# Down projection of the second and third token block by seven products of block sums, woven into the gate and up products

## Chip, core and metric

The kernel runs on one core of one Trainium2 chip. The time is the device time of one execution in microseconds (us); smaller is better. The program computes one layer of a decoder for a prompt of 2048 positions and a group of 32 sample rows (8 sequences of 4 positions).

## The reference, cut to what matters

The layer is attention beside a gating unit, an output projection with residual, and then a SwiGLU feed-forward part with residual, to which the change belongs:

```python
D_MODEL = 1024
D_FF = -(-8 * D_MODEL // (3 * 256)) * 256      # 2816

def _swiglu(x, g, w_gate, w_up, w_down):
    h = _rmsnorm(x, g)
    return (jax.nn.silu(h @ w_gate) * (h @ w_up)) @ w_down

def _layer_prompt(x, ...):
    ...
    x = x + jnp.concatenate([att, u * gate], axis=-1) @ w_out
    x = x + _swiglu(x, norm2_g, w_gate, w_up, w_down)
```

Everything is float32. `_layer_sample` does the same for the sample rows with the same weights, and a last RMSNorm follows. The caches of the sample group are copied to the outputs, shifted by the new positions.

## The kernel before

About the first 1000 us are projection and attention. The rest is done in three blocks of row tiles (a row tile is 128 positions): tiles 0 to 5, 6 to 11, and 12 to 15 with the sample rows. Each block first does the output projection and the second norm (the transition), and then the feed-forward part, in NF = 22 passes over f, each for 128 of the 2816 columns of `w_gate` and `w_up`.

**Precision.** A matmul operand is split into a high part (rounded to the matmul's float32 form) and a low part (the rest): `hi = copy(x)` on ScalarE (ACT), `lo = x - hi` on GpSimd (POOL) or VectorE (DVE). A product is three matmuls: high x high, high x low, low x high.

**Gate and up.** They are computed together as a 2x2 by 2x2 block product with seven products instead of eight (Strassen's way, in Winograd's form): rows in two halves of 64, `w_gate` and `w_up` against two halves of the inner dimension. For each f there are seven operand tiles (four blocks or sums of blocks of the weights), and seven `product(B, u, q)`, q = 0 to 6, of 12 matmuls each (4 parts k of the inner dimension, three matmuls each). They move 384 columns in block 2 (6 tiles x 64) and 272 in block 3 (4 tiles x 68, the sample rows with them). After a product, DVE or ACT combines its result from PSUM with earlier ones; silu stands on ACT after q = 2 and q = 5; after q = 6 `hidden` multiplies gate and up and splits the result as the stationary operand of the down projection. The first block forms the operand sums and keeps them in DRAM (`ab_d`); the others load them from there (`load_source`, tile names `fr`).

**The tick.** One product with what is issued behind it is a tick: `one(u, q)`. The order of all engines' instructions is that of the code (a manual schedule); each engine works its own queue in that order. In a tick of blocks 2 and 3, `prepare(B, f + 1, q)` issues for the next pass the low half of operand q - 1 (POOL, L1604), the high half of operand q (ACT, L1600) and the load of operand q of the pass after that (the SP queue). `later(n, ...)` puts work n ticks ahead.

**Down.** For each f, 128 rows of `w_down` are loaded into one row tile `fd` (`load_down`) and split into a pair `dw` (`split_down`, ACT L135 and POOL L138, 1024 wide). Two passes, an even and an odd f, make one `down_unit` for each row tile: for each of two 512-column halves 2 x 3 matmuls (L1743) into one PSUM bank and a DVE addition to the accumulator in SBUF (`acc`, L1745). These units stand in the ticks q = 3, 4 and 5 of the next even pass, two tiles each in block 2; the sample rows have a unit of 8 matmuls.

Of the kernel before, what the change touches and what calls it, by code (L numbers as in the profile page):

```python
# [19 lines left out]
P = 128  # L20
# [45 lines left out]
def hymba_step(ctx: ExitStack, tc: tile.TileContext, A: dict, O: dict):  # L66
# [53 lines left out]
    ab_d = dram.tile([NF, 7, P, 512], F32, name="ab_d")  # L120

# [1163 lines left out]
    def op_tile():  # L1285

        t_ = pool_["fg"].tile([P, 2, 512], F32R, name="op", tag="op", bufs=8)
        return t_[:, 0], t_[:, 1]
# [37 lines left out]
    class Block:  # L1326
# [9 lines left out]
        def place(self):  # L1336
            self.X = []
            for nm in ("xh2", "xl2"):
                t_ = fc.tile([P, 6 * 28 * 64], F32R, name=nm, tag=nm)
                self.X.append(t_[:, 0:self.nt * 28 * self.w].rearrange("p (i n) -> p i n", i=self.nt))  # L1340
            self.ops = [x.rearrange("p i (j k w) -> p i j k w", j=7, k=4) for x in self.X]
# [207 lines left out]
    ab, ops = {}, {}  # L1549
    POOL_LOW = (2, 4, 5)  # L1550
# [47 lines left out]
    def high(f, j):  # L1598
        ops[f, j] = op_tile()
# [6 lines left out]
    def both_halves(f, j):  # L1606
# [12 lines left out]
    EVEN_STAGES = (((both_halves, 0), (keep, 3)), ((both_halves, 1), (keep, 1)), ((both_halves, 2),), ((both_halves, 3),),  # L1619
                   ((sums, 5), (both_halves, 4)), ((both_halves, 5),), ((both_halves, 6), (keep, 5)), (), ())  # L1620
# [20 lines left out]
    def load_down(f):  # L1641
        raws["d", f] = w_ = pool_["fd"]
        sync.dma_start(w_, A["w_down"][f * P:(f + 1) * P, :])

# [6 lines left out]
    def product(B, u, q):  # L1651
# [9 lines left out]
        for k in range(4):  # L1661
# [3 lines left out]
            pe.matmul(out, wl[:, ks], xh[:, :, k], start=False, stop=(k == 3))  # L1665

# [28 lines left out]
        elif q == 6:  # L1695
            if a == 0:
# [16 lines left out]
    def hidden(B, u, zz, c):  # L1713

        f, a, b, g = u["f"], u["a"], u["b"], u["g", zz]
        dve.tensor_mul(g, g, c)  # L1716
# [9 lines left out]
        return lows  # L1726

# [102 lines left out]
    for s in range(KD):  # L1830
        at(L + (-12 if s < 4 else s - 14), "misc", lambda s=s: load_wo(0, s, lambda: first_stage(s)))
        at(L + (s - 11 if s < 4 else s - 10), "misc", split_wo, B, 0, s, lambda s: op_tile())
# [18 lines left out]
    gain.append(row_tile("final_g"))  # L1851
    pool_["fd"] = row_tile("fd")
# [24 lines left out]
    def first_operands(B):  # L1877
# [6 lines left out]
        later(6, load_down, 0)  # L1884
# [30 lines left out]
    def first_block(B):  # L1915
# [21 lines left out]
        def rest():  # L1937
# [3 lines left out]
            sync.dma_start(gain[0], dap(A["final_g"], 0, [[0, P], [1, D]]))  # L1941
# [33 lines left out]
    def next_block(B, downs, finals):  # L1975
# [15 lines left out]
        for s in (6, 7):  # L1991
            later(s - 5, split_wo, B, 0, s, lambda s: op_tile())
# [14 lines left out]
    for bi, B in enumerate(blocks):  # L2007
        if bi == 0:
# [10 lines left out]
        last_h = {}  # L2019

        def one(u, q):
            tick()
            product(B, u, q)
            f = u["f"]
# [5 lines left out]
            if f and q < 2:  # L2030
                prepare(B, f, 7 + q)
            if f + 1 < NF:
# [166 lines left out]
```

## Time and profile before

| | |
|---|---|
| time, median of 3 runs | 2595.95 us (2592.98 to 2599.67) |
| the profiled execution: time, span | 2594.14 us, 2592.3 us |
| TensorE (PE) busy, matmuls | 2467.8 us (95%), 13598 |
| weight loads (PEld) busy | 2175.4 us (84%) |
| DVE, ACT, POOL busy | 1430.4 us (55%), 1221.5 us (47%), 1369.7 us (53%) |
| mean granted TensorE clock | 0.985 |
| stages: feed-forward of block 1, 2, 3 | about 1030 to 1520, 1620 to 2100, 2200 to 2560 us |

How to read the profile: PE's matmuls are pipelined, so that one matmul's own length is longer than the distance to the next one's start; the distance is what it costs. In the views, `op<-fr` is an operation that writes tile `op` from tile `fr`; L1604 is line 1604 of the kernel; `[0.81 <-PE ps_m L1665]` is the idle time of that engine ahead of an operation and what ended it. Each engine takes its instructions in order, so an instruction that waits holds all behind it. In the groups by line, the numbers behind the second bar are the idle time ahead of the group and what ended most of it. SPq is the queue that issues DMA transfers.

### The profile page before, as it was taken

To read this page: it belongs to the slowest core of one execution; us is meant where nothing else is said; L and a number is where in the kernel's file an instruction comes from. 1 tells how busy PE (TensorE), PEld (TensorE's weight loads), DVE (VectorE), ACT (ScalarE), POOL (GpSimd) and SP (SyncE) were. 2 spreads that over 40 slices of the span, in tenths; PEclk is the share of its full clock that TensorE was granted. 3 is DMA by queue.
4 is the path that set the end of the run, shared out by engine and by line. 5 is a ranking of instruction groups with operands and counts; after the bars stand their busy time and mean duration, and the time that the engine had idled before them with its cause. 6 is when DMAs were issued, how large, how long until landed. Compare 5 with 4: busy or idle time off the path is not lost.

```text
span 2592.3 us, 38968 instructions
## 1 busy us (share of the span) xinstructions
PE 2467.8 (95%) x13598; PEld 2175.4 (84%) x13598; DVE 1430.4 (55%) x2783; ACT 1221.5 (47%) x2578; POOL 1369.7 (53%) x1068
## 2 busy tenths in 40 slices
PE   8998899999999889999999999999999999999996
PEld 6777776677988768898999988999999987999996
DVE  3359686345888877344444466544444457544445
ACT  5423335446878745554454545432332336444332
POOL 2035654123576745776776743554453634766662
PEclk9999999999999999999999999999999999999998
DMA  7764853588678674464564564455463643755553
GB/s 236 226 204 150 272 159 117 180 247 276 195 223 219 175 210 150 143 206 156 163 195 134 183 187 159 171 187 175 151 215 126 210 154 127 239 194 196 195 195 109
DMA packets 313409, 480.00 MB, mean 185 GB/s; under 512 B 25841, under 2 KB 178834, under 8 KB 307326
## 3 DMA queue, kind: packets, MB, share of 16 engines
q1 hardware_dynamic: 307740, 468.48, 56.7%
q10 hardware_dynamic: 5474, 9.04, 1.3%
q8 instruction: 108, 1.77, 0.3%
q14 instruction: 87, 0.71, 0.1%
HBM read 381.72 MB, written 165.83 MB: 211 GB/s over the span
## 4 chain that ended last, share of the span: by engine, by line
PE 36%; issue 8%; POOL 8%; DMA 4%; ACT 2%; DVE 2%; SPq 1%; POOLq 0%; ACTq 0%; DVEq 0%
PE ps_o L1743 12%; PE ps_m L1665 8%; PE ps_m L1663 8%; PE ps_m L1664 8%; POOL op L1604 2%; DMA ab_d<-pair 2%; ACT fr L1572 1%; POOL pair L1584 1%; POOL dw L138 1%; POOL fr L1587 1%; POOL pair L1593 1%; POOL pair L1590 1%; DMA out_yp_dram<-acc 1%; SPq L1390 1%; PE ps_o L1411 0%
## 5 line engine op out<-in xcount | busy, mean ns | idle before, releaser
L1604 POOL TENSOR_TENSOR op<-fr,op 128x512 fp32r<-128x512 f32 x385 | 488.6, 1298 | 285.1 <-ACT op L1600 273.9
L1665 PE MATMUL ps_m<-xh,op 128*128 128x384 f32 (+5 forms) x1932 | 610.8, 316 | 2.0 <-POOL op L1604 2.0
L1663 PE MATMUL ps_m<-xh,op 128*128 128x384 f32 (+5 forms) x1932 | 610.9, 316 | 0.0
L1664 PE MATMUL ps_m<-xl,op 128*128 128x384 f32 (+5 forms) x1932 | 609.8, 316 | 0.0
L1743 PE MATMUL ps_o<-dw,hw 128*128 128x512 f32 x2040 | 485.8, 393 | 14.8 <-DVE acc L1745 14.8
L1743 PEld LDWEIGHTS ps_o<-dw,hw 128*128 128x128 f32 x2040 | 380.5, 188 | 98.4 <-DVE acc L1745 21.9
L1663 PEld LDWEIGHTS ps_m<-xh,op 128*128 128x128 f32 x1932 | 364.2, 189 | 4.0
L1664 PEld LDWEIGHTS ps_m<-xl,op 128*128 128x128 f32 x1932 | 364.2, 189 | 3.5
L1665 PEld LDWEIGHTS ps_m<-xh,op 128*128 128x128 f32 x1932 | 364.1, 188 | 2.5 <-POOL op L1604 2.5
L1745 DVE TENSOR_TENSOR acc<-acc,ps_o 128x512 f32<-128x512 f32 (+1 forms) x362 | 247.1, 687 | 214.8 <-PE ps_o L1743 214.7
L1710 ACT ACTIVATE ps_t<-zn 128x384 f32<-128x384 f32 (+1 forms) x126 | 58.2, 462 | 463.9 <-DVE zn L1693 364.5
L1600 ACT ACTIVATE op<-fr 128x512 fp32r<-128x512 f32 x396 | 235.5, 623 | 20.8 <-DMA fr<-ab_d 18.1
L138 POOL TENSOR_TENSOR dw<-fd,dw 128x1024 fp32r<-128x1024 f32 x66 | 158.5, 2402 | 120.1 <-ACT dw L135 119.4
L318 PE MATMUL ps_s<-wh,xh 128*128 128x512 f32 x480 | 197.2, 411 | 6.1 <-ACT xh L135 6.0
L319 PE MATMUL ps_s<-wl,xh 128*128 128x512 f32 x480 | 191.7, 399 | 2.0 <-DVE wl L226 2.0
L320 PE MATMUL ps_s<-wh,xl 128*128 128x512 f32 x480 | 191.5, 399 | 0.0
L1604 POOL TENSOR_TENSOR op<-pair,op 128x512 fp32r<-128x512 f32 x63 | 81.2, 1297 | 117.1 <-ACT op L1600 117.1
L1720 ACT ACTIVATE hw<-ps_t 128x384 fp32r<-128x384 f32 (+1 forms) x126 | 56.1, 453 | 175.1 <-DVE ps_t L1716 174.1
L318 PEld LDWEIGHTS ps_s<-wh,xh 128*128 128x128 f32 x480 | 92.5, 193 | 35.9 <-issue 8.4
L319 PEld LDWEIGHTS ps_s<-wl,xh 128*128 128x128 f32 x480 | 92.8, 193 | 20.8 <-DVE wl L226 3.6
L320 PEld LDWEIGHTS ps_s<-wh,xl 128*128 128x128 f32 x480 | 92.2, 192 | 20.4 <-DVE xl L138 0.2
L135 ACT ACTIVATE dw<-fd 128x1024 fp32r<-128x1024 f32 x66 | 69.8, 1057 | 73.1 <-DMA fd<-in_w_down_dram 73.1
(489 smaller groups left out, 4769.6 us busy)
## 6 DMA issues: line engine op xcount, KB each, us to landing
fr<-ab_d SPq DMA_DIRECT2D x308, 256.0 KB
fd<-in_w_down_dram SPq DMA_DIRECT2D x66, 512.0 KB
out_ks_dram<-in_cache_k_dram SPq DMA_DIRECT2D x56, 512.0 KB
out_vs_dram<-in_cache_v_dram SPq DMA_DIRECT2D x56, 512.0 KB
ab_d<-fr SPq DMA_DIRECT2D x88, 256.0 KB
raw<-in_w_in_dram SPq DMA_DIRECT2D x72, 256.0 KB
qk_d<-pair SPq DMA_DIRECT2D x64, 256.0 KB
ab_d<-pair SPq DMA_DIRECT2D x63, 256.0 KB
```

Source lines behind the costliest of these rows:

```text
L135: act.activation(hi, src, AF.Copy)
L138: (eng_lo or pool).tensor_sub(lo, src, hi.bitcast(F32))
L318: pe.matmul(o[j], xh[:, k, :], wh, start=(k == 0), stop=False)
L319: pe.matmul(o[j], xh[:, k, :], wl, start=False, stop=False)
L320: pe.matmul(o[j], xl[:, k, :], wh, start=False, stop=(k == KD - 1))
L1600: act.activation(ops[f, j][0], ab[f][j], AF.Copy)
L1604: (pool if f or j in POOL_LOW else dve).tensor_sub(lo_, ab[f][j], hi.bitcast(F32))
L1663: pe.matmul(out, wh[:, ks], xh[:, :, k], start=(k == 0), stop=False)
L1664: pe.matmul(out, wh[:, ks], xl[:, :, k], start=False, stop=False)
L1665: pe.matmul(out, wl[:, ks], xh[:, :, k], start=False, stop=(k == 3))
L1743: pe.matmul(ps[0:nr], l_, r_[:, cs], start=(z == 0 and y == 0), stop=(z == FC - 1 and y == len(pairs) - 1))
L1745: dve.tensor_add(B.acc[i][0:nr, cs], B.acc[i][0:nr, cs], ps[0:nr])
```

## The change

From the second block on, the down projection is also made by seven products of block sums. The first block forms the sums of the blocks of `w_down` (`block_sums`, four DVE subtractions for each pair of passes) and keeps them in a DRAM tensor `td_d`; for this there are now two row tiles (`fd`, `fe`) instead of one and a separate one for the final gain, whose load moves to the end of each block. In blocks 2 and 3 a class `Seven` does the down projection of the pairs of passes 0 to 9; the last pair stays as it was.

A pair of passes gives 256 hidden rows, so the left side is 2x2 blocks (two row tiles by two passes) and the right side 2x2 blocks (two passes by two 512-column halves). `hidden` now multiplies gate and up on DVE into e1, e2 (even f) and o1, o2 (odd f), from which DVE forms sums; `put` splits the seven left blocks (high on ACT; low on DVE, for one block on POOL), `split` the seven right blocks (`d`, 512 wide: 0, 2 and 4 low on DVE, 1, 3, 5 and 6 low on POOL, and in block 3 also 7, for the sample rows). A step is 3 matmuls of 512 columns into a PSUM bank, in which products are added up, and a DVE addition of the bank to `acc` (7 for each pair of row tiles, where the units had 4). Two banks take turns.

In what follows, O0 to O6 are the ticks of an odd pass and E0 to E6 those of the even pass after it. The steps of a pair of passes are woven in from E3 on, one behind each part k of a product, so 4 in a tick: 21 in block 2 (to O1) and 14 with 4 for the sample rows in block 3 (to O0). The down units between the ticks are gone in blocks 2 and 3. `prepare` stands three ticks later there: the low half of operand j is issued three ticks ahead of the product that reads it. The operand buffers, a ring of 8, are a ring of 5 and one of 3 from which three right blocks are also taken.

```diff
-        t_ = pool_["fg"].tile([P, 2, 512], F32R, name="op", tag="op", bufs=8)
+        t_ = pool_["fg"].tile([P, 2, 512], F32R, name="op", tag="ox" if extra else "op", bufs=3 if extra else 5)
...
-    EVEN_STAGES = (((both_halves, 0), (keep, 3)), ((both_halves, 1), (keep, 1)), ((both_halves, 2),), ((both_halves, 3),),
-                   ((sums, 5), (both_halves, 4)), ((both_halves, 5),), ((both_halves, 6), (keep, 5)), (), ())
+    EVEN_STAGES = ((), ((both_halves, 0), (keep, 3)), ((both_halves, 1), (keep, 1)), ((both_halves, 2),), ((both_halves, 3),),
+                   ((sums, 5), (both_halves, 4)), ((both_halves, 5),), ((both_halves, 6), (keep, 5)), ())
...
+    def block_sums(g, part):
+        (t1, t3), (t4, t2) = ((r_[:, 0:512], r_[:, 512:1024]) for r_ in (rows2[1], rows2[0]))
+        if part == 0:
+            dve.tensor_sub(t1, t3, t1)
+        elif part == 1:
+            dve.tensor_sub(t3, t2, t3)
+            dve.tensor_sub(t2, t2, t1)
+            dve.tensor_sub(t4, t4, t2)
...
             pe.matmul(out, wl[:, ks], xh[:, :, k], start=False, stop=(k == 3))
+            if woven:
+                woven(k)
...
+        def split(self, eng, *ds):
+            for d in ds:
+                hi, lo_ = self.d[d]
+                act.activation(hi, self.raw(d), AF.Copy)
+                eng.tensor_sub(lo_, self.raw(d), hi.bitcast(F32))
+
+        def put(self, key, src, eng):
+            hi, lo_ = self.a[key]
+            act.activation(hi, src, AF.Copy)
+            eng.tensor_sub(lo_, src, hi.bitcast(F32))
...
+        def even(self, part):
+            e1, e2 = self.h[0]
+            if part == 0:
+                self.put("11", e1, dve)
+                self.h[2] = s3 = zn_tile()[:, 0:self.n]
+                dve.tensor_sub(s3, e1, e2)
+            else:
+                self.put("s3", self.h[2], dve)
+        def odd_a(self):
+            (e1, e2), (o1, o2) = self.h[0], self.h[1]
+            dve.tensor_sub(e1, e2, e1)
+            hi, lo_ = self.a["12"]
+            dve.tensor_sub(lo_, o1, hi.bitcast(F32))
+            self.put("s2", e1, dve)
...
+        STEPS = (("11", 0, 0, (0, 0)), ("12", 1, 1, (0, 0)), ("s2", 2, 0, (0, 1)), ("s1", 3, 1, (1, 1)), ("s3", 4, 0, (1, 1)),
+                 ("s4", 5, 1, (0, 1)), ("22", 6, 0, (1, 0)))
...
+        def one(self, p, banks, step):
...
+            for x, (l_, r_) in enumerate(((ah, dh), (ah, dl), (al, dh))):
+                pe.matmul(ps, l_, r_, start=(new and x == 0), stop=(x == 2), skip_group_check=True)
+            acc = self.B.acc[2 * p + par][:, half * 512:(half + 1) * 512]
+            dve.tensor_add(acc, acc, ps)
...
+        def plan(self, f, q):
+            g = f // 2
+            if f % 2 and g + 1 < NF // 2:
...
+                if q in (2, 3):
+                    self.even(q - 2)
+                if q in (1, 2, 4):
+                    self.load(g, *{1: (0, 1, 2, 3), 2: (4, 6), 4: (5, 7) if self.B.last else (5,)}[q])
+                for eng, ds in {2: ((dve, (0,)), (pool, (1,))), 3: ((dve, (2,)),), 4: ((pool, (3,)),),
+                                5: ((dve, (4,)),), 6: ((pool, (5,)),)}.get(q, ()):
+                    self.split(eng, *ds)
+            elif f % 2 == 0 and f:
+                if q == 0:
+                    self.split(pool, 6)
+                if q == 2 and self.B.last:
+                    self.split(pool, 7)
...
-            product(B, u, q)
+            product(B, u, q, st and st.woven(f, q))
+            if st and u["b"] == B.nt:
+                st.plan(f, q)
...
-            if f and q < 2:
-                prepare(B, f, 7 + q)
-            if f + 1 < NF:
-                prepare(B, f + 1, q)
+            if st:
+                if f and q < 5:
+                    prepare(B, f, 4 + q)
+                if f + 1 < NF and q > 2:
+                    prepare(B, f + 1, q - 3)
```

TensorE's queue in block 2 before, at a tick with two down units (L1743; `ps_o` are the down units' banks):

```order
L1663 MATMUL ps_m_16820<-xh_15482,op 128x384
L1664 MATMUL ps_m_16820<-xl_15483,op 128x384
L1665 MATMUL ps_m_16820<-xh_15482,op 128x384
L1743 MATMUL ps_o_16841<-dw,hw 128x512 x6
L1743 MATMUL ps_o_16849<-dw,hw 128x512 x6
L1743 MATMUL ps_o_16857<-dw,hw 128x512 x6
L1743 MATMUL ps_o_16865<-dw,hw 128x512 x6
L1663 MATMUL ps_m_16873<-xh_15482,op 128x384
```

and now, at E3 (`ao` and `pair` are left blocks; `op` and `db` right blocks):

```order
L1683 MATMUL ps_m_16920<-xh_15563,op 128x384
L1898 MATMUL ps_o_16924<-op,ao 128x512 x3
L1681 MATMUL ps_m_16920<-xh_15563,op 128x384
L1682 MATMUL ps_m_16920<-xl_15564,op 128x384
L1683 MATMUL ps_m_16920<-xh_15563,op 128x384
L1898 MATMUL ps_o_16932<-op,ao 128x512 x3
```

The down matmuls moved from between the products into them, three behind each part of a product.

POOL's queue in block 2 before, over two passes (L138 splits a row tile of `w_down`, L1604 is the low half of a gate and up operand):

```order
L1604 TENSOR_TENSOR op<-fr,op 128x512 x6
L138 TENSOR_TENSOR dw<-fd,dw 128x1024
L1604 TENSOR_TENSOR op<-fr,op 128x512 x4
L138 TENSOR_TENSOR dw<-fd,dw 128x1024
L1604 TENSOR_TENSOR op<-fr,op 128x512 x10
```

and now (L1607 is the low half of a gate and up operand, L1811 that of a right block, L1816 that of left block 22); the first L1811 is issued at O2, the last at E0:

```order
L1607 TENSOR_TENSOR op<-fr,op 128x512 x8
L1811 TENSOR_TENSOR op<-fd,op 128x512
L1607 TENSOR_TENSOR op<-fr,op 128x512 x2
L1811 TENSOR_TENSOR db<-db 128x512
L1607 TENSOR_TENSOR op<-fr,op 128x512 x2
L1811 TENSOR_TENSOR db<-fd,db 128x512
L1607 TENSOR_TENSOR op<-fr,op 128x512
L1811 TENSOR_TENSOR db<-db 128x512
L1607 TENSOR_TENSOR op<-fr,op 128x512
L1816 TENSOR_TENSOR ao<-zn,ao 128x384
```

Two long splits in a pair of passes became four short ones and a left block, which stand between the last low halves of the odd pass and the first five of the even one.

ACT's queue in block 2 at the same place, now, from O0 to O4 (L1693 takes the first product from PSUM, L1730 is silu, L1603 the high half of a gate and up operand, L1815 that of a left block, L1810 that of a right block):

```order
L1693 ACTIVATE zn<-ps_m_17945 128x384
L1603 ACTIVATE op<-fr 128x512 x2
L1730 ACTIVATE ps_t_18025<-zn 128x384
L1815 ACTIVATE ao<-fe 128x384
L1810 ACTIVATE op<-fd 128x512 x2
L1603 ACTIVATE op<-fr 128x512
L1815 ACTIVATE ao<-zn 128x384
L1810 ACTIVATE op<-op 128x512
```

where before stood, over the same ticks:

```order
L1673 ACTIVATE zn<-ps_m_17010 128x384
L1600 ACTIVATE op<-fr 128x512 x2
L1710 ACTIVATE ps_t_17065<-zn 128x384
L1600 ACTIVATE op<-fr 128x512 x2
L135 ACTIVATE dw<-fd 128x1024
L1600 ACTIVATE op<-fr 128x512
```

Behind silu, a left block and two right blocks now stand ahead of the next high half.

More of the change, by code (lines that the diff above doesn't have):

```diff
@@ L1598, in high @@
     def high(f, j):
-        ops[f, j] = op_tile()
+        ops[f, j] = op_tile(f == 0 and j > 4 if seven else j in (2, 5))
         act.activation(ops[f, j][0], ab[f][j], AF.Copy)
@@ L2018, in hymba_step @@
         rows = list(range(len(B.rows)))
-        last_h = {}
+        st = Seven(B) if bi else None
+        for u in units:
+            u["seven"] = st if u["f"] + 2 < NF else None
         def one(u, q):
+            f = u["f"]
             tick()
-            product(B, u, q)
-            f = u["f"]
+            if st and f and f % 2 == 0 and q == 3:
+                st.begin(f // 2 - 1)
+            product(B, u, q, st and st.woven(f, q))
+            if st and u["b"] == B.nt:
+                st.plan(f, q)
             if u["b"] < B.nt:
```

190 lines of the change are left out of this document (171 added, 19 removed).

## Prediction

> **What bounds the kernel now.** I read the busy time by stage first, then the timeline of TensorE in blocks 2 and 3, then the groups by line of those stretches. In the windows (stretch, its length, then PE, PEld, DVE, ACT, POOL busy us, granted clock, DMA share, GB/s; one row each from block 2 and block 3):
>
> ```profile
> 1700.00:1750.00 50.00, 50.00 (x267) 47.07 (x266) 22.38 (x39) 16.67 (x31) 26.72 (x21) 1.00 0.56 190
> 2300.00:2350.00 50.00, 50.00 (x328) 45.71 (x327) 24.82 (x54) 18.06 (x41) 26.70 (x19) 1.00 0.52 174
> ```
>
> PE has no gap there; the other engines are busy about half the time. What PE's time is made of, by the timeline (start, length, what):
>
> ```profile
> 1699.79 0.33 PE L1663 MATMUL ps_m<-xh,op 128*128 128x384 f32 x1
> ...
> 1707.42 0.33 PE L1665 MATMUL ps_m<-xh,op 128*128 128x384 f32 x1
> 1707.59 5.64 PE L1743 MATMUL ps_o<-dw,hw 128*128 128x512 f32 x24
> 1713.07 0.33 PE L1663 MATMUL ps_m<-xh,op 128*128 128x384 f32 x1
> ...
> 2306.10 0.29 PE L1663 MATMUL ps_m<-xh,op 128*128 128x272 f32 x1
> ...
> 2307.60 1.98 PE L1743 MATMUL ps_o<-dw,hs 128*64 128x512 f32 x8
> ```
>
> Starts are what counts. From 1699.79 to 1707.59 stand 45 matmuls: 173 ns each in block 2. The 24 down matmuls take 5.48 us: 228 ns each. In block 3, 12 gate and up matmuls fill 2306.10 to 2307.60: 125 ns each. So one of the seven products (12 matmuls, a tick) is 2.08 us in block 2 and 1.50 us in block 3, and a pair of passes 168 x 0.173 + 72 x 0.228 = 45.5 us in block 2, 168 x 0.125 + 56 x 0.228 = 33.8 us in block 3 (with the 8 of the sample rows).
>
> **What is removed.** Twelve matmuls for each row tile and pair of passes become 21 for two row tiles, so 3 are saved per pair of tiles: 9 in block 2 (2.05 us) and 6 in block 3 (1.37 us) for each of ten pairs of passes, 150 x 228 ns = 34.2 us. All of it is on the path, since PE has no gap. The sample rows stay at 8.
>
> **What is moved and added: the queues behind PE.** The groups by line of block 2 (line, engine, shapes, count, busy us, mean ns):
>
> ```profile
> L1604 POOL TENSOR_TENSOR op<-fr,op 128x512 fp32r<-128x512 f32 x136 | 172.5, 1299 | 153.4 <-ACT op L1600 143.9 <-DMA fr<-ab_d 8.9
> L1745 DVE TENSOR_TENSOR acc<-acc,ps_o 128x512 f32<-128x512 f32 x120 | 82.6, 688 | 80.0 <-PE ps_o L1743 80.0
> L1600 ACT ACTIVATE op<-fr 128x512 fp32r<-128x512 f32 x136 | 80.8, 622 | 0.6
> L1720 ACT ACTIVATE hw<-ps_t 128x384 fp32r<-128x384 f32 x40 | 19.7, 493 | 77.9 <-DVE ps_t L1716 77.1
> L1710 ACT ACTIVATE ps_t<-zn 128x384 f32<-128x384 f32 x39 | 19.4, 496 | 224.4 <-DVE zn L1693 172.0 <-DVE zn L1677 52.4
> L1677 DVE TENSOR_TENSOR zn<-zn,ps_m 128x384 f32<-128x384 f32 x19 | 10.5, 554 | 27.7 <-PE ps_m L1665 27.7
> ```
>
> and of block 3:
>
> ```profile
> L1716 DVE TENSOR_TENSOR ps_t<-ps_t,raw 128x272 f32<-128x272 f32 x40 | 17.8, 446 | 15.7 <-ACT ps_t L1710 15.0
> L1710 ACT ACTIVATE ps_t<-zn 128x272 f32<-128x272 f32 x40 | 15.9, 397 | 133.0 <-DVE zn L1693 115.2 <-DVE zn L1677 17.7
> L1720 ACT ACTIVATE hw<-ps_t 128x256 fp32r<-128x256 f32 x40 | 15.4, 385 | 27.5 <-DVE ps_t L1716 27.5
> L1677 DVE TENSOR_TENSOR zn<-zn,ps_m 128x272 f32<-128x272 f32 x20 | 8.8, 438 | 17.3 <-PE ps_m L1665 17.2
> L1324 DVE TENSOR_TENSOR hs<-ps_t,hs 128x16 fp32r<-128x16 f32 x38 | 6.3, 165 | 0.0
> L1716 DVE TENSOR_TENSOR raw<-raw,zn 128x136 f32<-128x136 f32 x1 | 0.3, 299 | 1.1 <-ACT raw L1710 1.1
> ```
>
> How POOL hangs on PE shows in this chain of block 3, begun by the product that ended at 2307.60:
>
> ```profile
> 2307.80 0.44 DVE L1693 TENSOR_TENSOR zn<-zn,ps_m 128x272 f32<-128x272 f32 x1 [0.81 <-PE ps_m L1665]
> 2308.27 0.40 ACT L1710 ACTIVATE ps_t<-zn 128x272 f32<-128x272 f32 x1 [10.73 <-DVE zn L1693]
> 2308.61 0.62 ACT L1600 ACTIVATE op<-fr 128x512 fp32r<-128x512 f32 x1
> 2309.30 1.29 POOL L1604 TENSOR_TENSOR op<-fr,op 128x512 fp32r<-128x512 f32 x1 [8.16 <-ACT op L1600]
> ```
>
> PE to DVE 0.20, then silu, then ACT's next high half, then POOL. Before, such a low half was used some six ticks later, and the down units, 5.5 us each, lay among those ticks. After, `prepare` runs three ticks later, so that a low half is issued three ticks ahead of its product; down splits stand before it in the same queues, and from O1 to E2 nothing is woven in: ticks of 2.08 and 1.50 us. I follow the last finisher at four places, block 2 / block 3.
>
> *O5 needs low half 5 at its third matmul.* After O2: 0.20 + add 0.554 / 0.438 + silu 0.496 / 0.397 + high half of block 11 0.493 / 0.385 + two split highs 1.24 + POOL's split and low half 5, 2 x 1.299 = 5.6 / 5.3. PE has two ticks and two matmuls, 26 x 0.173 or 0.125 = 4.5 / 3.25. Wait 1.1 / 2.0.
>
> *E0 needs low half 0.* Three POOL operations after low half 5, 3.90, against two ticks: 0 / 0.9.
>
> *E2 needs low half 2.* After O5: add, silu, split 4 on ACT and DVE (about 0.69, as an add) 2.56 / 2.35; the hidden products on DVE, two pairs of half size (128x136 took 299 ns and 128x272 446, so 0.36 / 0.29 each) and an add, with two small sample operations in block 3, 1.99 / 1.94; a small ACT step 0 / 0.17; ACT's block 12 and split 5, 1.11 / 1.01; POOL 2.60. Sum 8.3 / 8.1 against 38 matmuls, 6.6 / 4.75, and the 0.9 already waited. Wait 1.7 / 2.4.
>
> *E3 needs low half 3.* Two POOL operations 2.60 less one tick: 0.5 / 1.1.
>
> In block 2 the woven step at O0 also waits for DVE: the hidden work of E6 (1.99) stands before the add that frees its bank: 0.684 + 0.20 + 0.69 + 1.99 + 0.69 = 4.25 against 3.6 on PE, 0.6. Elsewhere a bank comes back in time: one 0.69 add against 1.2 us of PE.
>
> Together 3.9 / 6.4 us for a pair of passes, more than the 2.05 / 1.37 saved.
>
> **A price from another stage.** Nearly all the new DVE operations read two SBUF tiles; the removed and the kept ones read PSUM. Where such operations meet POOL:
>
> ```profile
> 957.14 0.68 DVE L1403 TENSOR_TENSOR xl<-xl,xh 128x512 fp32r<-128x512 f32 x1
> ...
> 959.45 3.47 DVE L138 TENSOR_TENSOR woh<-fr,woh 128x512 fp32r<-128x512 f32 x2
> ...
> 958.94 1.74 POOL L1086 TENSOR_TENSOR o<-o,zn 128x512 f32<-128x512 f32 x1
> ```
>
> 0.68 alone; in turns with POOL each takes 1.7, and POOL's 1.30 becomes 1.7 too. So every low half that meets one loses 0.40 (512 wide), by width 0.30 at 384 and 0.20 at 256. The bounds are 0 (they pass between POOL's operations) and 0.40; I take the width, since thirteen come for each pair of passes: six POOL operations in the waits of block 2, 1.8; eight in block 3, 1.6.
>
> **Transfers.** A 512 KB load in block 3:
>
> ```profile
> 2316.50 0.33 SPq L1643 DMA_DIRECT2D fd<-in_w_down_dram  x1
> ...
> 2320.03 1.06 ACT L135 ACTIVATE dw<-fd 128x1024 fp32r<-128x1024 f32 x1 [2.41 <-DMA fd<-in_w_down_dram]
> ```
>
> It landed 3.5 us after issue. The loads of O1 stand on SP behind an operand load that waits for low half 3: in block 3 that ends 5.4 us after E6's product (sample step 0.46, 0.20, add 0.69, hidden 1.94, 0.17, high 0.63, low 1.30), and the second down load, third in line, lands near 3.5 + 0.75 = 4.25 later, at 9.6. ACT wants it at 7.9 (0.46 + O0 2.41 + two ticks 3.0 + 2.05). Late by 1.7, on top of O5's wait; bounds 0 and 2.5. In block 2 the ticks are longer: 0. The 0.75 is 256 KB at this 350 GB/s:
>
> ```profile
> 1052.00:1055.50 3.50, 1.46 (x8) 1.00 0.36 87
> 1055.50:1059.00 3.50, 3.50 (x13) 0.51 1.04 350
> ```
>
> **The clock.** The same rows (PE alone): 2.0 us idle in 3.5, and in the next 3.5 us the granted clock is 0.51. The waits above reach 2 us. A half-clock stretch costs at most 1.7 us of matmuls, mostly in ticks where PE waits anyway; I take 0.5 for each pair of passes, 10 us; bounds 0 and 34. The Trainium skill ("TensorE: Matmul & The Clock Gate", section "HAM oscillation — how this bites in real kernels") puts the limit for idle gaps at about 3.4 us. By that rule these waits would cost nothing at the clock and the sum would be 10 lower; the row shows a shorter idle enough.
>
> **Block 1.** Four DVE subtractions and 1 MB of stores a pair of passes. Three stand ahead of O5's add (L1693), which releases silu and the hidden products, and the second also waits until POOL has split the rows it overwrites:
>
> ```profile
> 1153.19 0.55 DVE L1693 TENSOR_TENSOR zn<-zn,ps_m 128x384 f32<-128x384 f32 x1 [0.94 <-PE ps_m L1665]
> 1154.09 2.41 POOL L138 TENSOR_TENSOR dw<-fd,dw 128x1024 fp32r<-128x1024 f32 x1
> 1161.16 1.02 DVE L1324 TENSOR_TENSOR hw<-ps_t,hw 128x384 fp32r<-128x384 f32 x2 [4.74 <-ACT hw L1720]
> ```
>
> 3 x 1.7 = 5.2 us against the 4.74 that DVE idles afterwards: 0.5 a pair, 5 us; bounds -8 (the shifted even stages relieve ACT) and +20. The earlier weight load, the ring of operand buffers cut in five and three, and the later load of the final gain keep four or more ticks of cover: 0; without it, one DMA landing each, 3.5.
>
> **Sum.** Block 2: 3.9 + 1.8 - 2.05 = 3.65 x 10 = 36. Block 3: 6.4 + 1.6 + 1.7 - 1.37 = 8.3 x 10 = 83. Clock 10, block 1 5. The profiled execution took 2594.1 us (2592.3 span), 1.8 below the median of three runs: 2594 + 134 = 2728.
>
> **Rivals.**
> *The count decides.* POOL reaches each low half before PE does, so the 34.2 us stay: 2560. For it: POOL's 27 of 50 busy. Against it: it decides only if after O2 the four ACT steps and two POOL operations fit into 4.5 / 3.25 us, and they add up to 5.6 / 5.3. Chance 0.07.
> *The queues wait, but nothing else does.* No turns with POOL, loads in time, full clock, block 1 even: 18 + 50 more, 2663. For it: the turns are seen in another stage. Chance 0.14.
> *DVE and transfers are the bound.* Every two-tile operation costs 0.40 and loads of O4 are late as well, 0.8 in block 3, clock and block 1 at their upper bounds: about 2728 + 6 + 8 + 24 + 15 = 2781, more if waits add up. Chance 0.09 for over 2790.
> *The forecast*, 0.70.
>
> **How the numbers follow.** Prediction 2728. The low end is the second rival, 2663; the high end 2790. The first rival, part of the second and what lies above are left out, 0.2. A change under 0.3% (8 us) can't be told from none. Faster 0.07, same 0.02, slower 0.91.
>
> **What would show it.** Right: PE waits of 1 to 4 us in each pair of passes of blocks 2 and 3, at a third matmul and released by POOL's low half (L1607); block 2 near 49 us and block 3 near 42 for a pair, from 45.5 and 33.8; DVE's two-tile operations (L1811, L1816) at 1 us or more; half-clock stretches in both blocks. Wrong: PE without gaps there, or waits released by DVE's adds (L1900).

## The result and the profile after

The changed kernel takes **2739.14 us** (median of 4 runs, 2732.99 to 2743.46) against 2594.47 (4 runs, 2592.8 to 2599.67): ratio 1.0552, 95% interval 1.0522 to 1.0583. The prediction was 2728 with a range of 2663 to 2790. The profiled execution took 2734.9 us, its span 2733.1.

The windows of blocks 2 and 3 of the changed kernel (stretch, length, busy us of PE, PEld, DVE, ACT, POOL, then granted clock, DMA share, GB/s):

```profile
1640.00:2140.00 500.00, 458.47 (x2310) 417.14 (x2310) 353.28 (x557) 172.54 (x340) 267.73 (x192) 0.98 0.53 172
2240.00:2640.00 400.00, 329.45 (x1924) 302.22 (x1923) 267.77 (x519) 151.29 (x346) 229.94 (x180) 0.88 0.55 177
```

PE now has 41.5 us of gaps in 500 of block 2 and 70.6 in 400 of block 3, where before it had none (PE had no wait between its matmuls in the feed-forward part of either block). Who ends them, by the waits of PE in the same two stretches (us in total, times, longest):

```profile
PE ps_m L1683 <- POOL op L1607: 40.9, 25, 2.9
...
PE ps_m L1683 <- POOL op L1607: 70.5, 21, 5.2
```

All of them are the third matmul of a product (L1683) waiting for POOL's low half, as forecast; none is DVE's add. The length of a pair of passes is the distance between first matmuls of two odd passes, here in block 2 and in block 3:

```profile
1769.69 0.34 PE L1681 MATMUL ps_m<-xh,op 128*128 128x384 f32 x1
...
1819.27 0.34 PE L1681 MATMUL ps_m<-xh,op 128*128 128x384 f32 x1
...
2326.92 0.29 PE L1681 MATMUL ps_m<-xh,op 128*128 128x272 f32 x1
...
2371.34 0.29 PE L1681 MATMUL ps_m<-xh,op 128*128 128x272 f32 x1
```

These two pairs took 49.6 and 44.4 us. In the tables below stands the mean over the second to the ninth pair of a block (the first and last also hold the start and the end of the weaving), and the block's length from its first gate and up matmul to its last, all from the profiled execution:

| | block 1 | block 2 | block 3 | pair in 2 | pair in 3 |
|---|---|---|---|---|---|
| before | 510.7 | 491.2 | 369.9 | 45.6 | 34.0 |
| changed | 496.0 | 536.5 | 483.8 | 50.0 | 45.0 |
| difference | -14.7 | +45.3 | +113.9 | +4.4 | +11.0 |

The sum is +144.5; with -3.7 outside the three blocks it is the 140.8 between the two profiled executions (2734.9 and 2594.1).

One wait of block 3, at O5, by rows of the timeline (those of the chain alone):

```profile
2376.43 1.50 SPq L1805 DMA_DIRECT2D fd<-in_w_down_dram  x2
...
2377.82 0.40 ACT L1815 ACTIVATE ao<-fe 128x256 fp32r<-128x256 f32 x1
2380.45 0.63 ACT L1810 ACTIVATE op<-fd 128x512 fp32r<-128x512 f32 x1 [2.23 <-DMA fd<-in_w_down_dram]
2381.51 0.63 ACT L1810 ACTIVATE op<-fd 128x512 fp32r<-128x512 f32 x1 [0.42 <-DMA fd<-in_w_down_dram]
2382.04 0.61 ACT L1603 ACTIVATE op<-fr 128x512 fp32r<-128x512 f32 x1
2382.21 1.27 POOL L1811 TENSOR_TENSOR op<-fd,op 128x512 fp32r<-128x512 f32 x1 [4.93 <-ACT op L1810]
2383.44 3.14 POOL L1607 TENSOR_TENSOR op<-fr,op 128x512 fp32r<-128x512 f32 x2
...
2384.95 0.60 PE L1683 MATMUL ps_m<-xh,op 128*128 128x272 f32 x1 [4.70 <-POOL op L1607]
```

Read it upwards from PE: POOL's low half of operand 5 stands behind the split of right block 1, that behind ACT's high half, and ACT stood 2.65 us for the two loads that SP issued at 2376.43. Behind the wait PE runs at half clock (the matmul's 0.60 us, where the same matmul took 0.29 at 2371.34): such stretches make the 0.88 of block 3's window.

### The profile page after: what moved, and what is told of

Read it like the earlier page. It is cut to its first block, busy times and chain, and to the rows that moved or that the text cites. A ratio compares the mean times of both kernels' runs of the same rounds, so it can differ in the third digit from the quotient of the medians.

```text
span 2733.1 us, 39993 instructions
## 1 busy us (share of the span) xinstructions
PE 2496.4 (91%) x13448; PEld 2194.9 (80%) x13448; DVE 1772.7 (65%) x3275; ACT 1286.2 (47%) x2744; POOL 1457.0 (53%) x1138
## 4 chain that ended last, share of the span: by engine, by line
PE 32%; issue 11%; POOL 9%; DMA 5%; DVE 4%; ACT 2%; SPq 0%; POOLq 0%; ACTq 0%; DVEq 0%
POOL op L1607 7%; PE ps_m L1683 6%; PE ps_o L1961 6%; PE ps_m L1682 6%; PE ps_m L1681 6%; PE ps_o L1898 5%; DMA fd<-in_w_down_dram 3%; DMA fr<-ab_d 1%; DMA db<-td_d 1%; POOL db L1811 0%; DVE acc L1963 0%; POOL op L1811 0%; PE ps_o L1413 0%; PE ps_o L1415 0%; PE ps_o L1414 0%
## 5 line engine op out<-in xcount | busy, mean ns | idle before, releaser
L1683 PE MATMUL ps_m<-xh,op 128*128 128x384 f32 (+5 forms) x1932 | 638.8, 331 | 125.4 <-POOL op L1607 125.3
L1607 POOL TENSOR_TENSOR op<-fr,op 128x512 fp32r<-128x512 f32 x385 | 524.2, 1378 | 311.5 <-ACT op L1603 307.6
L1681 PE MATMUL ps_m<-xh,op 128*128 128x384 f32 (+5 forms) x1932 | 628.0, 325 | 0.3 <-DVE raw L1711 0.3
L1682 PE MATMUL ps_m<-xl,op 128*128 128x384 f32 (+5 forms) x1932 | 628.2, 325 | 0.0
L1683 PEld LDWEIGHTS ps_m<-xh,op 128*128 128x128 f32 x1932 | 381.8, 198 | 142.0 <-POOL op L1607 140.8
L1681 PEld LDWEIGHTS ps_m<-xh,op 128*128 128x128 f32 x1932 | 381.4, 197 | 21.5 <-issue 0.6
L1682 PEld LDWEIGHTS ps_m<-xl,op 128*128 128x128 f32 x1932 | 380.9, 197 | 17.8
L1900 DVE TENSOR_TENSOR acc<-acc,ps_o 128x512 f32<-128x512 f32 x350 | 239.7, 687 | 127.8 <-PE ps_o L1898 123.8
L1730 ACT ACTIVATE ps_t<-zn 128x384 f32<-128x384 f32 (+1 forms) x126 | 58.6, 465 | 507.6 <-DVE zn L1713 360.3
L1603 ACT ACTIVATE op<-fr 128x512 fp32r<-128x512 f32 x396 | 237.4, 619 | 43.9 <-PE ps_m L1683 37.0
L1961 PE MATMUL ps_o<-dw,hw 128*128 128x512 f32 x840 | 199.3, 392 | 5.5 <-DVE acc L1963 5.5
L1961 PEld LDWEIGHTS ps_o<-dw,hw 128*128 128x128 f32 x840 | 156.6, 188 | 40.2 <-DVE acc L1963 8.8
L1963 DVE TENSOR_TENSOR acc<-acc,ps_o 128x512 f32<-128x512 f32 x142 | 96.7, 686 | 80.8 <-PE ps_o L1961 80.8
L1607 POOL TENSOR_TENSOR op<-pair,op 128x512 fp32r<-128x512 f32 x63 | 86.2, 1376 | 97.9 <-ACT op L1603 52.9
L1898 PE MATMUL ps_o<-op,ao 128*128 128x512 f32 x450 | 133.1, 406 | 0.0
L612 POOL TENSOR_TENSOR vl<-kv,vh 100x512 fp32r<-100x512 f32 (+1 forms) x32 | 45.9, 1438 | 109.3 <-PE ps_t L622 37.0
```

The costliest lines, as they stand in the source:

```text
L1603: act.activation(ops[f, j][0], ab[f][j], AF.Copy)
L1607: (pool if f or j in POOL_LOW else dve).tensor_sub(lo_, ab[f][j], hi.bitcast(F32))
L1681: pe.matmul(out, wh[:, ks], xh[:, :, k], start=(k == 0), stop=False)
L1682: pe.matmul(out, wh[:, ks], xl[:, :, k], start=False, stop=False)
L1898: pe.matmul(ps, l_, r_, start=(new and x == 0), stop=(x == 2), skip_group_check=True)
L1900: dve.tensor_add(acc, acc, ps)
```

## The experiments

Each is the changed kernel with one edit, unless it says otherwise; where an expectation says so, work is left out. Times are medians, ratios are to the kernel before (95% interval).

| run | time, us | ratio | block 2 | block 3 | pair in 2 | pair in 3 |
|---|---|---|---|---|---|---|
| changed | 2739.1 | 1.0552 (1.0522 to 1.0583) | 536.5 | 483.8 | 50.0 | 45.0 |
| no operands | 2573.5 | 0.9925 (0.9900 to 0.9950) | 484.0 | 376.8 | 44.2 | 32.7 |
| no right blocks | 2585.8 | 0.9973 (0.9959 to 0.9987) | 485.2 | 385.7 | 44.3 | 33.7 |
| no loads | 2701.8 | 1.0419 (1.0393 to 1.0446) | 528.6 | 451.5 | 49.2 | 41.0 |
| no left lows | 2723.3 | 1.0500 (1.0474 to 1.0525) | 521.6 | 485.8 | 48.3 | 44.9 |
| filled waits | 2728.6 | 1.0520 (1.0489 to 1.0552) | 531.0 | 476.0 | 49.5 | 44.4 |
| silu behind | 2702.7 | 1.0423 (1.0406 to 1.0441) | 500.3 | 481.6 | 46.0 | 44.7 |
| longer lead | 2714.0 | 1.0472 (1.0450 to 1.0494) | 526.2 | 466.8 | 49.1 | 43.3 |
| no POOL splits | 2657.9 | 1.0246 (1.0229 to 1.0263) | 494.0 | 447.5 | 45.3 | 40.8 |
| before, shifted | 2576.5 | 0.9941 (0.9927 to 0.9954) | 491.2 | 369.6 | 45.6 | 34.0 |
| plain downs | 2574.7 | 0.9931 (0.9918 to 0.9943) | 491.2 | 369.6 | 45.6 | 34.0 |
| seven in block 2, new order | 2573.4 | 0.9923 (0.9911 to 0.9935) | 488.4 | 369.6 | 44.8 | 34.0 |
| seven in both, new order | 2643.1 | 1.0195 (1.0170 to 1.0220) | 487.2 | 435.8 | 44.8 | 39.8 |

**Is it the queues?** *No operands:* `later(1, odd_a)` and its fellows, `even`, `load` and `split` run only for the first pair.

```diff
-            if f % FC and zz == 0:
+            if f == 1 and zz == 0:
                 later(1, self.odd_a)
...
-                    self.split(eng, *ds)
+                    if g == 0:
+                        self.split(eng, *ds)
```

> Leaves out: from the second pair of passes of blocks 2 and 3 on, no operand block of the woven products is made (no load, no split of a right block, no left block, no block sum of the hidden rows); the woven matmuls read what the first pair left, so down products are wrong. PE's programme is that of the changed kernel. Theory (queues: PE waits because these operations stand on ACT, DVE and POOL ahead of POOL's low halves): all waits of blocks 2 and 3 go, each pair falls to the matmul count, 45.5 - 2.05 = 43.5 us and 33.8 - 1.4 = 32.5 us, from 50.1 and about 44.8; the clock goes back to 1.0; span 2733 - 9 x 6.6 - 9 x 12.3 = about 2563. Rival (the shorter lead of three ticks itself is too short: add, silu, high and low half alone): PE still waits on L1607 in both blocks and the span stays over 2650. Rival (the woven matmuls wait for DVE's adds): waits on the adds of L1900 appear, span over 2600.

Pairs of 44.2 and 32.7, no wait in the eight middle pairs of either block. The waits of PE from 1640 to 2080 us, one in the first pair (at 1642) and one in the last (at 2075):

```profile
PE ps_m L1683 <- POOL op L1607: 3.5, 2, 2.1
```

So the three ticks of lead are enough for the gate and up operands alone, and the woven matmuls wait for nobody: the rivals fall. It is also the price list of the count: 1.4 us a pair saved in block 2, 1.2 in block 3, where the prediction had 2.05 and 1.37. In block 2 a woven step costs (4.89 - 2.08) / 4 = 0.70 us, by the lengths of E3 and O2, rather than 3 x 0.228, and O0 is 0.3 longer than E3.

*No right blocks:* the same two conditions on `load` and `split` alone.

> Leaves out: loads and splits of the right blocks (L1805, L1810, L1811) from the second pair of passes of blocks 2 and 3 on; left blocks are made as in the changed kernel. Theory (POOL's splits and ACT's split highs ahead of the low halves are the larger part of the waits; without them the chain after O2 is 0.20 + 0.55 + 0.50 + 0.49 + 0.62 + 1.30 = 3.7 us against 4.5 in block 2 and 3.0 against 3.25 in block 3): nearly all waits go, pairs near 43.5 to 45 and 32.5 to 35, span 2565 to 2600. Rival (DVE's work on the left blocks, in turns with POOL, sets the waits): at least half of them stay, span over 2650.

Pairs of 44.3 and 33.7: the right blocks are the waits, nearly all of them. The left blocks cost 1.0 us a pair in block 3, and there the wait is another, at E3, by the waits of PE from 2200 to 2600 us of this run:

```profile
PE ps_o L1898 <- DVE acc L1900: 7.1, 9, 1.1
```

**Which part of the right blocks?** *No loads:* `for d in ds if g == 0 else ():` in `load`.

> Leaves out: only the loads of the right blocks (L1805) from the second pair of passes of blocks 2 and 3 on; the splits are still made, of stale rows. Theory of the prediction (second load of O1 late by 1.7 us in block 3, in time in block 2): block 3 shorter by 10 to 17 us, block 2 unchanged, 2739 to about 2724. Rival (the loads land in time, the wait is POOL's and ACT's own work): within 5 us of 2739. Rival (loads also hold up the operand loads behind them on SP): 30 us or more shorter, in both blocks.

Block 3 is 32 us shorter, 4.0 a pair, and block 2 eight, 0.8 a pair: more than the theory's 17 and 0. O5 of block 3 falls from 7.45 to 3.89 us on the mean. The waits for loads on ACT in block 3 (2240 to 2640 us; the changed kernel, then this run) and in block 2 of the changed kernel (1640 to 2140 us) go with it: in block 3 twice a pair, 2.6 us together, in block 2 once, 0.8.

```profile
ACT op L1810 <- DMA fd<-in_w_down_dram: 23.4, 18, 2.2
...
ACT op L1810 <- DMA fd<-in_w_down_dram: 2.8, 2, 1.6
...
ACT db L1810 <- DMA fd<-in_w_down_dram: 7.0, 9, 1.3
```

The numbers of the second rival came out (over 30 us, both blocks), but not its mechanism: in these two stretches of the changed kernel none of ACT's high halves (L1603) waits for an operand load.

*No POOL splits:* POOL's `tensor_sub` of `split` left out after the first pair.

> Leaves out: POOL's low halves of the right blocks (L1811, four a pair in block 2, five in block 3) after the first pair; ACT's high halves, DVE's low halves and the loads stay. Theory (POOL's queue: each stands ahead of one or two low halves that PE needs, 1.3 us at O5, E2 and E3): waits of block 2 fall to under 1 us a pair, block 2 shorter by 25 to 35 us; block 3 by 25 to 45 us, the late transfer at O5 stays; 2739 to 2660 to 2690. Rival (ACT's split highs, which wait for transfers, are what holds POOL up): less than 25 us shorter in all.

81 us shorter, 42 in block 2 and 36 in block 3. Block 2 is nearly without waits (1.0 us a pair is left, at E3), with ACT's split highs and the loads still there: there the waits go with the four splits in POOL's queue. The theory was right in kind, its 25 to 35 for block 2 too low. In block 3 6.8 us a pair are left over the plain kernel.

**Is it turns of DVE and POOL?** *No left lows:* DVE's `tensor_sub` of `put` and of block 12 left out after the first pair.

> Leaves out: the low halves of the left blocks that DVE makes (six two-tile operations, 384 or 256 wide, of each pair of passes; L1816 and that of block 12) after the first pair. Theory (DVE and POOL take turns: six of thirteen such operations, so about half of the 1.8 and 1.6 us): mean of L1607 falls from 1378 to about 1340 ns, span shorter by 10 to 20 us in both blocks together, 2739 to about 2722. Rival (turns cost nothing on the path): within 5 us. Rival (DVE's queue is the bound): 40 us or more shorter.

15 us in block 2, nothing in block 3. The groups of POOL's low half from 1640 to 2100 us, of the changed kernel and of this run:

```profile
L1607 POOL TENSOR_TENSOR op<-fr,op 128x512 fp32r<-128x512 f32 x129 | 181.7, 1428 | 139.3 <-ACT op L1603 139.3
...
L1607 POOL TENSOR_TENSOR op<-fr,op 128x512 fp32r<-128x512 f32 x135 | 180.7, 1359 | 143.4 <-ACT op L1603 143.4
```

1428 ns became 1359; alone it is 1.30 us. DVE pays the other side, by its groups of the changed kernel in block 2 (alone, and in turns):

```profile
L1811 DVE TENSOR_TENSOR op<-fd,op 128x512 fp32r<-128x512 f32 x9 | 6.2, 685 | 0.0
...
L1811 DVE TENSOR_TENSOR op<-op 128x512 fp32r<-128x512 f32 x9 | 15.8, 1754 | 0.0
```

Half of the two-tile operations were taken away and 1.7 us a pair of block 2 went, as much as the prediction had for all. It is not a pure measure of the turns: DVE's queue became shorter as well. In block 3 O5, where the loads come last, stays at 7.5 us, and what E2 loses (0.6) E3 takes in large part (0.4). The Trainium skill ("GPSIMD Engine Reference", section "1. Specifications") names this contention of POOL with DVE operations that have two SBUF inputs; the trace agrees, 685 ns against 1754.

**Is it the clock?** *Filled waits:* matmuls ahead of the third one of O5 and E2.

```diff
+            if k == 0 and fill:
+                dummy = bank(2)
+                for _ in range(fill):
+                    pe.matmul(dummy[:, 0:n + lead * B.w].rearrange("p (i w) -> p i w", w=B.w), wh[:, ks], xh[:, :, k], start=True, stop=True)
             pe.matmul(out, wl[:, ks], xh[:, :, k], start=False, stop=(k == 3))
```

> Adds matmuls that nobody reads (into a free bank, ahead of the third matmul of the product, that is inside the wait for POOL): 6 at O5 and 8 at E2 in block 2 (1.0 and 1.4 us at 0.173), 24 at O5 and 12 at E2 in block 3 (3.0 and 1.5 us at 0.125). Theory (the half clock that follows a wait delays the products behind it and through them the queues, about 5 us for a pair of block 3): the half-clock stretches of block 3 mostly go, clock above 0.95 there, span shorter by 20 to 45 us. Rival (the half clock falls into ticks in which PE waits for POOL anyway, as the prediction took it): within 8 us of 2739. Rival (waits are shorter than the filling): up to 30 us longer.

The window of block 3 in this run:

```profile
2240.00:2640.00 400.00, 351.59 (x2290) 321.44 (x2291) 272.89 (x533) 155.18 (x355) 236.90 (x182) 0.99 0.55 179
```

The clock is back from 0.88 to 0.99 and the time is not: block 3 is 8 us shorter, block 2 five (in the profiled execution, the fastest of four), the medians 10.6 apart with intervals that overlap. The filling itself cost no time: in every pair from the second on, the third matmul still waited for POOL behind it. With full clock PE reaches the next missing operand sooner and waits there: of block 3's ticks O6, behind the wait at O5, falls from 2.58 to 1.79 us, and E0 rises from 1.55 to 2.12. So the half clock, for all its share of the window, is worth about 0.5 us a pair, as the prediction had put it.

**Is it order or amount?** *Silu behind:* on ACT, silu and the high half of block 12 go behind the operand halves of their tick.

```diff
+            elif u["seven"]:
+                behind.append(gate)
...
-            u["g", 1] = silu_of(u, 1, c12)
+            def up():
+                u["g", 1] = silu_of(u, 1, c12)
+
+            behind.append(up) if u["seven"] and b == B.nt else up()
...
-                act.activation(self.a["12"][0], o1, AF.Copy)
+                behind.append(lambda: act.activation(self.a["12"][0], o1, AF.Copy))
...
                     prepare(B, f + 1, q - 3)
+                while behind:
+                    behind.pop(0)()
```

> Same work; on ACT the silu of products 2 and 5 and the high half of block 12 are issued behind the split and high halves of their tick instead of ahead of them, so ACT's highs no longer wait for the end of that product and DVE's add. Theory (the chains at O5 and E2 begin with a product's end, 0.20 + add + silu = 1.25 / 1.03 us each, and in order issue alone ties POOL to it): up to 2.5 us a pair less in block 2, 2 in block 3, if transfers allow; 2739 to 2700 to 2720, block 2 more than block 3. Rival (POOL's and ACT's total work between O2 and E3 is the limit, whatever the order): within 8 us.

Block 2: 36 us shorter, more than the upper bound of the theory (25); block 3 only two, of up to 20 expected: there the loads, not silu, come last at O5 (ACT's waits for them are 36.5 us here from 2240 to 2600 us). All the work of block 2 is still there; the waits at O5 (1.75) and E2 (2.95 over its 2.08) are gone and E3 keeps 1.7. The waits of PE from 1640 to 2100 us, where the changed kernel has 39.5 us in 24:

```profile
PE ps_m L1683 <- POOL op L1607: 17.6, 13, 2.0
```

With the amount of work unchanged, ACT's order alone makes most of block 2's waits: silu, waiting for a product's end and DVE's add, stood in front of high halves whose inputs had long been there. It is a chain through ACT and then POOL, so taking POOL's splits out of it (above) removed these waits as well.

*Longer lead:* `prepare(B, f, 5 + q)` for q < 4 and `prepare(B, f + 1, q - 2)` for q > 1.

> Same work; the operands are prepared two ticks behind the loads' plan instead of three (one tick earlier, as far as the ring of five buffers lets it). Theory (lead is short: each of O5, E0, E2, E3 gains up to one tick, 2.08 / 1.5 us, less where the high half now waits for the buffer's last reader): 2739 to 2700 to 2725. Rival (the ring gives nothing: with five buffers the high half waits for the product just issued): within 8 us. Rival (ACT then waits for PE and everything behind is later): longer.

25 us, within what was expected. O5 and E2 of block 2 are without a wait, but E3 is 9.5 us long instead of 5.9: the wait moves on more than it goes. Three waits are new or longer there from 1640 to 2100 us: PE's for DVE's adds (L1900, 13.0 us), and those of ACT's high halves for products that still read the ring's buffers (39.1 us, 13.6 in the changed kernel) and for operand loads (21.6). What each of them costs was not separated.

**Block 1.** *Before, shifted:* the kernel before with the new `EVEN_STAGES` alone.

> The kernel before with one line of the change: in block 1 the operand stages of the even passes begin one tick later. Theory (block 1's 14.7 us come from it: ACT's and POOL's operand work no longer meets the first woven unit at E3): block 1 from 510.7 to about 496, all else as before, 2594 to about 2580. Rival (the gain comes from the ring cut in five and three, or from the weight load placed earlier): block 1 stays at 510, within 3 us of 2594.

Block 1 takes 497.4 us, 13.3 less, so this one line is nearly the whole gain of block 1 (the span is 20 shorter; the other 7 lie ahead of block 1, where nothing was edited). PE's waits of block 1, in the kernel before and here:

```profile
PE ps_o L1743 <- DVE acc L1745: 10.8, 10, 3.0
...
PE ps_o L1743 <- DVE acc L1745: 2.6, 2, 1.9
```

In the kernel before, ACT's copy of E0's product (L1673) came behind the high halves and twice eight gain scalings of the two ticks before, ahead of which ACT had waited 3.5 us for an operand sum of POOL (L1593; 1.0 at the same place in the shifted kernel). DVE's chain began late, and the first down unit's add (L1745) with it (rows of the chain alone):

```profile
1111.05 0.63 ACT L1600 ACTIVATE op<-pair 128x512 fp32r<-128x512 f32 x1 [3.52 <-POOL pair L1593]
1111.59 2.44 ACT L1572 ACTIVATE fr<-fr,g2c 128x128 f32<-128x128 f32 x8
1113.93 0.85 ACT L1720 ACTIVATE hw<-ps_t 128x384 fp32r<-128x384 f32 x2
1114.67 0.62 ACT L1600 ACTIVATE op<-fr 128x512 fp32r<-128x512 f32 x1
1115.19 2.45 ACT L1572 ACTIVATE fr<-fr,g2c 128x128 f32<-128x128 f32 x8
1117.54 0.48 ACT L1673 ACTIVATE zn<-ps_m 128x384 f32<-128x384 f32 x1
...
1118.05 0.56 DVE L1675 TENSOR_TENSOR raw<-zn,ps_m 128x384 f32<-128x384 f32 x1 [2.59 <-ACT zn L1673]
1119.65 1.28 DVE L1745 TENSOR_TENSOR acc<-acc,ps_o 128x512 f32<-128x512 f32 x2
1120.38 3.01 PE L1743 MATMUL ps_o<-dw,hw 128*128 128x512 f32 x12 [0.81 <-DVE acc L1745]
```

**What can be had.** *Plain downs:* the changed kernel with `st = None`, `seven` left empty and `block_sums` in block 1 only, so all of block 1's part and no seven products.

> The changed kernel without the seven products: block 1 with its new stages, loads, rings, block sums and their stores, blocks 2 and 3 with the twelve matmuls of the kernel before. Theory (the price lies in blocks 2 and 3 alone, 45.3 and 113.9 us): block 1 496, block 2 491, block 3 370, about 2578 to 2582, faster than before by 0.5%. Rival (rings of five and three buffers cost block 2 or 3 something as well): over 2590.

As expected: 2574.7. Block sums, stores and rings cost block 1 nothing (495.9 against 497.4 with the shift alone).

*Seven in block 2, new order:* silu behind, plain block 3, and in block 2

```diff
+                    loads = {0: (2, 3), 1: (4, 6), 2: (5,)}
+                    splits = {0: ((dve, (0,)), (pool, (1,))), 1: ((dve, (2,)),), 2: ((pool, (3,)),), 4: ((dve, (4,)),)}
...
+                if f > 2 and q in (0, 2):
+                    self.split(pool, 5 + q // 2)
...
+                if g + 1 < NF // 2 and q == 5:
+                    self.load(g, 0, 1)
```

> Seven products in block 2 only, block 3 as in the kernel before, block 1 of the change. In block 2 from the second pair on: silu behind the operand halves (as in the run where that was done alone), the raw right blocks 0 and 1 loaded two ticks before the end of the pair before, splits two ticks earlier (0 and 1 at O0, 2 at O1, 3 at O2, 4 at O4, 5 at E0, 6 at E2). Theory (with the waits gone only the matmul count is left: 44.2 us a pair was the run without operands, 46.0 the one with silu behind): pairs of 44.2 to 45.2, block 2 484 to 493, time 2572 to 2582. Rival (any order gives about 46, waits move to another low half): block 2 500, time 2588.

Pairs of 44.8, block 2 488.4: here the seven products are faster than the twelve, by 2.8 us of a block. The time, 2573.4, is the lowest of the kernels that leave nothing out and beats both the kernel before and the changed one. But nearly all of its gain over the kernel before is that of block 1's shift (2576.5), and from the plain downs' 2574.7 it can't be told (the intervals overlap).

*Seven in both, new order:*

> The changed kernel with the order of the previous run (silu behind, raw blocks loaded ahead of the next pair, splits earlier) in block 3 as well as in block 2; same work, seven products in both. Theory (in block 3 a pair leaves 32.7 us by count, and the kernel before 33.9; between O2 and E3 POOL, in turns with DVE, and ACT have more to do than PE's ticks of 1.5 us last, so no order hides it; late transfers are only a third of it): block 2 488, block 3 pairs of 39 to 42 and 425 to 455 us, time 2630 to 2665. Rival (order and transfers are all of it, as in block 2): block 3 pairs under 35, time under 2590. Rival (the silu's order matters only in block 2 and transfers only through O5: gains of the single runs add up, 32 + 2): block 3 450, upper end of the theory.

Block 3 is 48 us shorter than in the changed kernel and still 66 longer than the plain one. POOL there, in the timeline from O2 of one pair on (O3 begins at 2313.30, E3 at 2327.47):

```profile
2312.55 1.29 POOL L1816 TENSOR_TENSOR op<-fd,op 128x512 fp32r<-128x512 f32 x1 [11.18 <-ACT op L1815]
2313.80 3.15 POOL L1607 TENSOR_TENSOR op<-fr,op 128x512 fp32r<-128x512 f32 x2
2316.91 1.47 POOL L1816 TENSOR_TENSOR db<-db 128x512 fp32r<-128x512 f32 x1
2318.35 6.90 POOL L1607 TENSOR_TENSOR op<-fr,op 128x512 fp32r<-128x512 f32 x5
2327.33 1.28 POOL L1816 TENSOR_TENSOR db<-fd,db 128x512 fp32r<-128x512 f32 x1 [2.08 <-ACT db L1815]
```

It works 12.7 us without a gap on seven low halves and two splits, where the seven ticks from O3 to E2 are 10.5 us of PE's own work, after it had stood idle for 11.2 behind ACT's high half of a right block. In block 3 the work is thus crowded into the ticks without weaving, and the ticks with it have a hole. Whether more operand buffers would let POOL fill the hole was not tried; that the rest of block 3's loss goes away with it stays open.

## Why the prediction was right, and where not

**The time** was 11 us off (0.4%), but by two errors of opposite sign: block 1 was taken 20 us too dear, blocks 2 and 3 some 30 too cheap (129 forecast with the clock, 159 measured). That the two nearly cancel is luck. Term by term, for a pair of passes of block 2 / block 3:

| term | predicted | measured, and from what |
|---|---|---|
| matmuls saved | 2.05 / 1.37 | 1.4 / 1.2: before less no operands |
| waits, turns, late transfer, clock | 6.2 / 10.2 | 5.8 / 12.2: changed less no operands |
| of it the late transfer | 0 / 1.7 | 0.8 / 4.0: no loads |
| of it the clock | 0.5 / 0.5 | 0.5 / 0.6: filled waits |
| of it turns | 1.8 / 1.6 | 1.7 / 0 for half of the operations, DVE's shorter queue included |

*What bounds, and the mechanism:* right. PE waits at the third matmul for L1607, in both blocks, and not for L1900; without the queued work the waits are gone. One sign held in part only: of DVE's two-tile splits (L1811, L1816), forecast at 1 us or more, the means in block 2 lie between 0.69 and 1.75 us. The weight of block 2's chain lay where the prediction had begun it, at silu.

*The places:* O5 waited 1.75 in block 2 (1.1 predicted, before turns), E2 2.95 (1.7), E3 1.0 (0.5), E0 nothing (0). In block 3 O5 is 5.9 us over its tick (2.0 and the late load's 1.7 predicted), O6 behind it 1.1 (mostly half clock), E2 4.2 (2.4), E3 1.0 (1.1). E0 had 0.9 predicted and nothing measured: the longer wait at O5 let POOL catch up, for without the loads, with O5 at 3.89, E0 is 0.8 over its tick.

*The late transfer* is the term of blocks 2 and 3 that was mis-sized. The loads were issued when forecast: O0 begins at 2371.34, the last gate and up matmul of E6 ended some 0.45 earlier, and 2376.43 is 5.5 us behind that, against 5.4. But they took 4.0 and 5.1 us to land instead of 3.5 and 4.25, and ACT waits for both, 2.65 us in the pair shown. A load late on top of a wait was priced by its own lateness, 1.7; ACT's waits for loads are 2.6 a pair, and without the loads O5 alone falls by 3.6. What the rest of the 4.0 is was not separated.

*The clock* was sized right and for the right reason, that half-clock time falls into ticks where PE would wait anyway. The clock row of block 3, 0.88, tempts one to charge it 400 x 0.12 = 48 us; the filled waits show 8. The Trainium skill ("TensorE: Matmul & The Clock Gate", section "HAM oscillation — how this bites in real kernels"), which the prediction weighed, sets the harm at idle gaps above some 3.4 us; waits of 2 to 3 us did halve the clock in block 2, so the measurement decides against that limit, though the time hardly noticed.

*Block 1* is the step that failed: +5 predicted, -14.7 measured, beyond the lower bound of -8. The subtractions of the block sums, priced at three turns against DVE's idle time, cost nothing: block 1 takes 495.9 us with them (plain downs) and 497.4 without (before, shifted). And the relief by the later even stages was left in the bounds, though PE's ten waits for L1745 and the tick of some 8.7 us at E3, against 7.6 in block 2, stood in the profile of before. They were not read, because the stage looked full: PE was busy.

*The rivals:* "the count decides" describes the run without operands, 2573; "the queues wait but nothing else" fails by the transfers (4.0 us a pair of block 3) and, in block 2, as far as the run without left lows measures them, the turns; "DVE and transfers are the bound" was right on the transfers in block 3 and wrong on the clock.

## What to carry to other kernels

Matmuls saved are paid for by whoever makes their operands: count what each queue has to do between two uses, in the ticks where it must be done, before counting matmuls, and a shorter tick (1.5 against 2.08 us) makes the same work unhideable. In an in-order queue, put an operation that waits for the newest result behind those whose inputs are already there: that alone gave back 36 of 45 us in block 2. A stretch at half clock is no loss by itself if the engine would stand at the next wait; fill it and look.

## What was not expected of the hardware

The half clock does not follow from the length of a gap alone. In the changed kernel the half-clock stretches of blocks 2 and 3 begin at whole multiples of 3.413 us from one another. The windows on that grid, two and two (an idle stretch and the one behind it):

```profile
1894.64:1898.05 3.41, 1.53 (x9) 1.54 (x10) 3.41 (x3) 3.04 (x7) 3.41 (x4) 1.00 0.16 45
1898.05:1901.46 3.41, 3.24 (x10) 2.43 (x9) 2.42 (x4) 0.96 (x3) 3.41 (x3) 0.50 0.27 94
1993.63:1997.04 3.41, 1.76 (x10) 1.44 (x9) 3.41 (x4) 3.41 (x8) 3.41 (x3) 1.00 0.60 216
1997.04:2000.45 3.41, 2.65 (x14) 2.24 (x14) 3.41 (x4) 0.62 (x2) 3.41 (x3) 1.00 0.33 77
```

1.88 us of idle PE in one window halves the clock of the next (0.50); 1.65 does not (1.00). No window of blocks 2 and 3 in this execution lies between: those at full clock that half clock followed had 1.88 us idle or more, the others 1.65 or less. In the other runs the border is less sharp (without POOL's splits, a window with 1.64 was followed by half clock; in both blocks, new order, one with 1.85 was not). A wait of 2.2 us that is cut by a window's border goes unpunished: the one of 2.23 us that ends at 1796.80 leaves 1.08 and 1.15 us idle in its two windows, and the clock stays at 1.00. That is why block 2, with a wait of 1.7 to 2.9 us at E2 in every pair, has a half-clock stretch in only some of them. The Trainium skill ("TensorE: Matmul & The Clock Gate", section "What's actually happening") says that activity is judged in windows of 3413 ns that run freely; the grid of the trace agrees.
